# Weight forms kept over a change of token half, a down projection in alternating thirds, and new constants of the planner

## The chip, the cores and the metric

The kernel runs on one core of a Trainium2 chip. The metric is the device time of one execution in microseconds (us), given as the median of several runs. The engines are TensorE (PE, with its weight loads listed apart as PEld), VectorE (DVE), ScalarE (ACT), GpSimd (POOL) and SyncE (SP), which issues nearly all the DMAs of this kernel.

## The reference, cut to what matters

One decoder block over 2048 tokens and 1024 channels, in float32:

```python
u = rms_norm(h, norm1_gain)
x_lru, g_lru, q, k, v, g_ret = split(u @ w_in)            # 1024 x 3072
y_lru = rms_norm(rg_lru(conv4(x_lru)) * gelu(g_lru))      # a scan along the tokens
y_ret = head_group_norm(retention(rotary(q), rotary(k), v)) * silu(g_ret)
h = h + concat(y_lru, y_ret) @ w_out                      # 1024 x 1024
a, b = split(conv3(rms_norm(h, norm2_gain) @ ffn_up_w))   # 1024 x 6144, conv along the tokens
h = h + (gelu(a) * b) @ ffn_down_w                        # 3072 x 1024
return rms_norm(h, final_norm_gain)
```

## The kernel before, in words

**Tiling.** Activations are held transposed, channels on the 128 partitions and tokens along the free axis. The 2048 tokens are two halves of 1024 (`HT`), called g = 0 and g = 1. Work goes through stages: A and AS (input projection), B (output projection), U (up projection) and D (down projection, whose 3072 inputs are cut into three thirds, c = 0, 1, 2, each of which adds to the residual). `order` near the end of the kernel lists the stages: A and AS of half 0, AS of half 1, B of both halves, U of both, then the thirds 0, 1, 2 of D for half 0 and the thirds 0, 1, 2 for half 1.

**Units.** A stage is a list of units. A unit takes two weight tiles of 128 x 1024 (`wsrc`) and makes two output tiles of 128 x 1024. `PlainUnit` does this in eight products of twelve matmuls; `Unit` does it in seven, with sums and differences of weight quarters and of activation blocks (a Strassen form; `PRODUCTS` lists them). Each float32 operand is split into a high part (an ACT cast to fp32r) and a low part (a DVE subtraction), and each product sums high x high, high x low and low x high. `Unit.weights` loads the two tiles (`wa`, `wb`), forms the sums (`s`) on DVE, and splits them: it makes the forms a, s1, s2 and v, seven slots of 4 KB per partition. Every unit of every half does this afresh, so each weight tile is loaded and split twice, once per half. After a product that uses a form last, `free` gives its slots back. The last unit of the last stage is a `LastUnit`, a plain unit whose columns are cut finer at the end.

**Outputs.** A unit's sums leave PSUM through `PlainOut` (ACT copies; stages A and U) or `AddOut` (DVE additions onto a residual tile that was loaded; stages B and D). Then the chains of the stage go on: `LruOut` (conv, gates on TensorE, `pa` and `pg`, then sigmoid, exp, tanh, sqrt on ACT, a scan on DVE and, when all four LRU units of a half are done, `LruGroup` with the `mst` matmuls over `sqacc`), `QkOut` and `VgOut` (rotary and retention), `UpOut` (conv and gelu; two neighbouring channels j are put together in `even[0]` and written as blocks to DRAM), `NormGroup` (a norm over the eight output tiles of a half).

**What sets the order.** The program is written out by a planner in Python, `Flow`. Every chain is a generator that yields one engine operation at a time; the planner keeps a clock for each engine and for the DMAs with costs of its own, and at each step issues, on the engine that can start first, the ready operation of the lowest rank. The order on each engine is then fixed. Time is counted in ticks: each product of the main chain has a tick, a `Unit` has period 7. Its constants: `SOON` is by how many ticks a chain that empties PSUM is due earlier than its nominal time; `NEAR` and `RESERVE` hold back the last four SBUF slots (of `SLOTS` = 55) from chains that are due later; `BACKLOG` is how many us of DMA work may be queued; `XS` says how long ahead of a half its normalised input is made; `CL` stands in the rank:

```python
def rank(self, tick):
    return self.prio if self.feeds or tick > 10 ** 5 else max(self.prio, tick - CL)
```

`prio` is the due tick. The chains that feed TensorE (`main`, `bring`, `weights`) keep it. With CL = 100 practically every other chain keeps it too, so the longer one is overdue, the lower its rank and the sooner it goes.

**Around the change.** `ORDER` lists the units of stage A for each half: `l3` is LRU unit 3, `q0` and `v0` the two units of retention head 0. `stage_b`, `stage_u` and `stage_d` build the unit lists in ascending order for both halves. `Stage.bring` loads the activation blocks of a stage and splits them (`raw`, `bh`).

Of the kernel before, what the change touches and what calls it, by code (L numbers as in the profile page):

```python
# [32 lines left out]
KT = D // P  # L33
# [5 lines left out]
NF = DFF // P  # L39
# [1 line left out]
SLOTS = 55  # L41
BANKS = {"x": 1, "y": 2, "e": 2, "sm": 3}
RESERVE = 4
NEAR = 3
BACKLOG = 10.0
SMALL = 150
ORDER = ("l0 q0 v0 l1 q1 v1 l2 q2 v2 l3 q3 v3", "l0 q0 v0 l1 q1 v1 q2 v2 l2 q3 v3 l3")
RATE = 330.0
LATE = 16
PLAIN = 4  # L50
SOON = 1.5
WB = 2
CH = 4
ISSUE = 0.45
CL = 100
NDUE = 3
LESS = 0
XSTEP = 6
XD0 = 10
XS = 60  # L60
XD = 50
RAW = 4
LEAD = 12
# [264 lines left out]
def hymba_block_kernel(ctx: ExitStack, tc: tile.TileContext, xh, xn, win, wout, wup, down, gates, vecs,  # L328
# [3 lines left out]
    NG = S // HT  # L332
# [15 lines left out]
    free = fl.free  # L348
# [240 lines left out]
    class Unit:  # L589
# [6 lines left out]
        def __init__(self, stage, wsrc, out):  # L596
            self.stage, self.wsrc, self.out = stage, wsrc, out
            self.w = {}
            self.there = {n: Event() for n in ("a", "s1", "s2", "v")}
            self.done = {n: Event() for n in ("seed", "u2", "c11", "c22a", "c22b")}  # L600
            out.unit = self

        def weights(self, t0):
            self.t0 = t0
# [64 lines left out]
        def p1(self):  # L669
# [7 lines left out]

            fl.spawn(seed(), self.t0 - 3 - SOON)

# [8 lines left out]

        def p2(self):
            yield from self.product(self.x, "a", "12", "21", False)  # L690
            free(*self.w["a"])
            fl.spawn(self.out.c11(), self.t0 + 1.9 - SOON)

        def p7(self):
            yield self.done["u2"]
            yield from self.product(self.y, "s1", "3", "T3", False)
            free(*self.w["s1"])
            fl.spawn(self.out.c22(), self.t0 + 2.5 - SOON)

        def p4(self):  # L700
            yield self.done["c22a"]
            yield from self.product(self.y, "v", "v", "T4", False)
            free(self.w["v"])
            fl.spawn(self.out.c21(), self.t0 + 6 - LESS)

        def p3(self):
            yield self.done["c22b"]
            yield from self.product(self.e, "s2", "4", "22", False)
            free(*self.w["s2"])
            fl.spawn(self.out.c12(), self.t0 + 8 - LESS)  # L710

    class PlainUnit:


        period = 8
        quads = ((0, 0), (0, 1), (1, 0), (1, 1))
# [4 lines left out]
        def __init__(self, stage, wsrc, out):  # L721
            self.stage, self.wsrc, self.out = stage, wsrc, out
            self.w = {}
            self.there = [[Event(), Event()] for m in range(2)]
            self.placed = [Event(), Event()]
            out.unit = self
            out.quads = {}

# [48 lines left out]
        def part(self, q, m, n, k, c0=None, c1=None):  # L777
            if c0 is None:
                c0, c1 = n * Q, (n + 1) * Q
            if k == 0:  # L780
                PlainUnit.count += 1
                self.ps = yield Bank(self.tags[PlainUnit.count % 5], "pq")
            yield self.there[m][k]
            bname = f"{k + 1}{n + 1}"
            wh, wl = self.w[m]
            op = None
            for j in range(4):
                if j % 2 == 0:
                    yield self.stage.event(bname, j // 2)
                bh, bl = self.stage.blk[bname, j // 2]  # L790
                c = slice(j % 2 * Q + c0 - n * Q, j % 2 * Q + c1 - n * Q)
                ws = slice((4 * k + j) * P, (4 * k + j + 1) * P)
                for i, (x, y) in enumerate(((wh, bh), (wh, bl), (wl, bh))):
                    mm = pe.matmul(self.ps[:, 0:c1 - c0], x[:, ws], y[:, c], start=k == 0 and j == 0 and i == 0,
                                   stop=k == 1 and j == 3 and i == 2)
                    op = op + mm if op else mm
                if self.halves:
                    yield op
                    op = None
            if op:  # L800
                yield op
            self.stage.used(bname)
            if k == 1:
                if m not in [x[0] for x in self.quads[q + 1:]]:
                    free(*self.w[m])
                fl.spawn(self.leave(m, n, c0, c1), self.t0 + 2 * q + 4 - SOON)

        def leave(self, m, n, c0, c1):
# [665 lines left out]
    class UpOut(PlainOut):  # L1474
# [22 lines left out]
        def first(self):  # L1497
            t0 = self.unit.t0
            yield t0 + 11
            ca = yield from self.conv(self.t1, self.j)  # L1500
            yield a.activation(ca, ca, AF.Gelu_apprx_tanh)
            yield self.there
            yield v.tensor_tensor(out=ca, in0=ca, in1=self.cv, op=ALU.mult)
            free(self.cv)
            if self.j % 2 == 0:
                even[0] = ca
            else:
                yield t0 + 14
                yield from g_d[self.g][self.j // 8].put(self.j // 2 % 4, even[0], ca)

    even = [None]


    def stage_a(g):
# [24 lines left out]
    def stage_b(g):  # L1539
        st = RawStage("B", g, m_d[g])  # L1540
        ng = NormGroup(V_N2, u_d[g].put, h_d[g][0], LATE * g)
        us = []
        for m in range(KT // 2):
            ms = (m, m + KT // 2)
            src = [(x_d[g][k // 2], k % 2) for k in ms]
            us.append(PlainUnit(st, (wout[ms[0]], wout[ms[1]]), AddOut(src, lambda i, t, ms=ms: ng.add(ms[i], t))))
        return st, us

    def stage_u(g):
        st = Stage("U", g, u_d[g])  # L1550
        return st, [Unit(st, (wup[j], wup[NF + j]), UpOut(g, j)) for j in range(NF)]

    def stage_d(g, c):
        st = Stage("D", g, g_d[g][c])
        final = g == NG - 1 and c == 2

        def store(q, *pair):
            for j in range(2):
                m = 2 * q + j
                yield dma(yT[m * P:(m + 1) * P, g * HT:(g + 1) * HT], pair[j])  # L1560
                free(pair[j])

        ng = FinalGroup(V_NF, None) if final else NormGroup(V_NF, store, h_d[g][3])

        def partial(m, t):
            yield from h_d[g][c + 1][m // 2].put(m % 2, t)
            free(t)

        us = []
        for m in range(KT // 2):  # L1570
            ms = (m, m + KT // 2)
            src = [(h_d[g][c][k // 2], k % 2) for k in ms]
            done = (lambda i, t, ms=ms: ng.add(ms[i], t)) if c == 2 else (lambda i, t, ms=ms: partial(ms[i], t))
            out = AddOut(src, done)
            out.pieces = lambda i, t, c0, c1, ms=ms: ng.piece(ms[i], t, c0, c1)
            kind = LastUnit if final and m == KT // 2 - 1 else Unit
            us.append(kind(st, (down[c, ms[0]], down[c, ms[1]]), out))
        return st, us

    order = sum((stage_a(g) for g in range(NG)), []) + [stage_b(g) for g in range(NG)] + [stage_u(g) for g in range(NG)]  # L1580
    order += [stage_d(g, c) for g in range(NG) for c in range(3)]

    def vectors():
        yield dma(gain1, vecs[:, V_N1:V_N1 + KT], "a")
# [3 lines left out]
    with tc.manual_schedule():  # L1588
        fl.spawn(setup(), -60)
        fl.spawn(vectors(), -50)  # L1590
        fl.spawn(constants(), 3)
        table = {}
        end = 0
        last = None
        for i, (st, us) in enumerate(order):
            if last is PlainUnit and type(us[0]) is Unit:
                end += 4
            if st.kind == "A":
                norm1(0, -200, end + NDUE)
                make_x(0, 0, end + XD0)  # L1600
            elif st.kind == "AS" and st.g:
                norm1(st.g, end - 70, end - 60)
                make_x(st.g, end - XS, end - XD)
            for j, u in enumerate(us):
                if type(u) is PlainUnit and last is Unit:
                    end += 0
                elif type(u) is Unit and last is PlainUnit and j:
                    end += 4
                last = type(u)
                u.weights(end)  # L1610
                if isinstance(u.out, AddOut):
                    u.out.load(end)
                for dt, name, block in u.products:
                    assert end + dt not in table
                    table[end + dt] = getattr(u, name)
                    st.uses(block, end + dt)
                end += u.period
            st.prepare(STAGE_LEAD if i else 300)

        def main():  # L1620
            for tick in sorted(table):
                yield tick
                fl.tick = tick
                yield from table[tick]()
            fl.tick = 10 ** 6

        fl.spawn(main(), -4)
        fl.run()
# [69 lines left out]
```

## Time and profile before

| what | us |
|---|---|
| median of 3 runs | 2182.34 (2181.40 to 2182.86) |
| profiled execution, its own time | 2183.93 |
| its span, first to last instruction | 2182.1 |
| TensorE busy in it | 2152.2 |
| VectorE busy in it | 1764.3 |
| ScalarE busy in it | 1245.9 |

The profile is of one execution. In its views "busy" is the time in which an engine has an instruction at work; a row of waits names who waited, for whom, the us in total, how many times, and the longest; the granted clock is a share of TensorE's full 2.4 GHz, so 0.50 is 1.2 GHz. The chain of waits is followed back from the last instruction. Matmuls are pipelined: the mean duration of one is longer than the distance from one to the next.

### The profile page before, as it was taken

The numbers are of one execution on the slowest core, as the hardware profiler recorded it, in microseconds if no ns is written. First come the engines' busy times: TensorE is split into PE (matmuls) and PEld (weight loads), VectorE is DVE, ScalarE is ACT, GpSimd is POOL, SyncE is SP. The second block draws the span as 40 slices with busy tenths as digits, with TensorE's granted clock in tenths as the row PEclk, the third lists the DMA queues.
The fourth block names the chain that finished last, engine by engine and source line by source line (L and its number), as shares of the span: only waits on it lengthen the run. The fifth ranks groups of instructions, "written<-read, shape, count | busy, mean of one in ns | idle before, by whom it ended". The sixth has DMA issues, their size and how long they took to land.

```text
span 2182.1 us, 26589 instructions
## 1 busy us (share of the span) xinstructions
PE 2152.2 (99%) x9848; PEld 1773.1 (81%) x9848; DVE 1764.3 (81%) x2227; ACT 1245.9 (57%) x1792; POOL 39.3 (2%) x32
## 2 busy tenths in 40 slices
PE   9999989999999999999999999999999999999998
PEld 6878878888788888888888888888888788888787
DVE  6999888877765688898888898788878987788875
ACT  6774775654852166666666766666666553343441
POOL 0010000000000000000000000000000000000000
PEclk9999999999999999999999999999999999999999
DMA  8966365142647954453224532322335787689662
GB/s 323 373 228 207 109 222 167 61 137 70 224 164 263 374 191 167 166 177 130 100 91 155 193 121 97 116 90 97 112 118 177 264 314 254 227 295 398 230 255 78
DMA packets 142498, 411.00 MB, mean 188 GB/s; under 512 B 16112, under 2 KB 20640, under 8 KB 142368
## 3 DMA queue, kind: packets, MB, share of 16 engines
q1 hardware_dynamic: 141072, 408.25, 52.8%
q8 instruction: 77, 1.26, 0.2%
q10 hardware_dynamic: 1296, 1.05, 0.1%
q14 instruction: 53, 0.43, 0.1%
HBM read 275.78 MB, written 125.07 MB: 184 GB/s over the span
## 4 chain that ended last, share of the span: by engine, by line
PE 94%; DVE 3%; DMA 2%; ACT 1%; POOL 0%; issue 0%; SPq 0%; DVEq 0%
PE py L127 33%; PE px L127 22%; PE pe L127 22%; PE pq L127 12%; PE po L127 1%; DMA raw<-in_dram 1%; PE pa L127 1%; PE pt L127 1%; PE pk L127 1%; PE sc L127 1%; DVE raw L127 1%; PE mst L127 1%; DMA xt<-in_dram 0%; DVE res L127 0%; DMA h<-h 0%
## 5 line engine op out<-in xcount | busy, mean ns | idle before, releaser
L127 DVE TENSOR_TENSOR wl<-s,wh 128x1024 fp32r<-128x1024 f32 x182 | 222.2, 1221 | 108.8 <-ACT wh L127 106.5
L127 PE MATMUL px<-bh,wh 128*128 128x512 f32 x728 | 287.2, 395 | 0.4 <-DVE res L127 0.4
L127 PE MATMUL py<-bh,wl 128*128 128x512 f32 x728 | 284.0, 390 | 2.8 <-DVE wl L127 2.8
L127 PE MATMUL px<-raw,wh 128*128 128x512 f32 x728 | 285.0, 391 | 0.3 <-DVE raw L127 0.3
L127 PE MATMUL py<-bh,wh 128*128 128x512 f32 x728 | 285.2, 392 | 0.0
L127 PE MATMUL pe<-raw,wh 128*128 128x512 f32 x728 | 283.4, 389 | 1.6 <-DVE raw L127 1.6
L127 PE MATMUL pe<-bh,wh 128*128 128x512 f32 x728 | 284.8, 391 | 0.0
L127 PE MATMUL px<-bh,wl 128*128 128x512 f32 x728 | 284.7, 391 | 0.0
L127 PE MATMUL py<-raw,wh 128*128 128x512 f32 x728 | 283.8, 390 | 0.3 <-DVE raw L127 0.3
L127 PE MATMUL pe<-bh,wl 128*128 128x512 f32 x728 | 283.5, 389 | 0.0
L127 ACT CAST wh<-s 128x1024 fp32r<-128x1024 f32 x182 | 190.9, 1049 | 140.8 <-DVE s L127 127.2
L127 DVE SCALAR_TENSOR_TENSOR c<-o,vec,c 128x1022 f32<-128x1022 f32 x192 | 244.1, 1279 | 9.0 <-ACT c L127 4.6
L127 PE MATMUL py<-bh,wv 128*128 128x512 f32 x728 | 240.4, 391 | 3.4 <-ACT o L127 1.7
L127 ACT COPY o<-py 128x512 f32<-128x512 f32 x204 | 119.6, 587 | 198.1 <-PE py L127 197.7
L127 DVE TENSOR_TENSOR raw<-raw,bh 128x1024 fp32r<-128x1024 f32 x158 | 189.2, 1217 | 7.0 <-ACT bh L127 7.0
L127 ACT CAST bh<-raw 128x1024 fp32r<-128x1024 f32 x158 | 161.5, 1048 | 35.7 <-DMA raw<-g_T 14.4
L127 PE MATMUL pq<-bh,wh 128*128 128x512 f32 (+1 forms) x432 | 168.0, 389 | 0.5 <-ACT bh L127 0.4
L127 PEld LDWEIGHTS px<-bh,wh 128*128 128x128 f32 x728 | 137.8, 189 | 35.3 <-issue 3.8
L127 PE MATMUL pq<-bh,wl 128*128 128x512 f32 (+1 forms) x432 | 165.0, 382 | 0.5 <-DVE wl L127 0.5
L127 PEld LDWEIGHTS py<-bh,wv 128*128 128x128 f32 x728 | 136.7, 188 | 34.1 <-ACT o L127 2.2
L127 PEld LDWEIGHTS py<-bh,wl 128*128 128x128 f32 x728 | 136.8, 188 | 31.8 <-DVE wl L127 3.2
L127 PEld LDWEIGHTS px<-bh,wl 128*128 128x128 f32 x728 | 137.5, 189 | 29.0
(143 smaller groups left out, 3819.1 us busy)
## 6 DMA issues: line engine op xcount, KB each, us to landing
wa<-in_dram SPq DMA_DIRECT2D x91, 512.0 KB, 4.6
wb<-in_dram SPq DMA_DIRECT2D x91, 512.0 KB, 5.2
h<-res SPq DMA_DIRECT2D x56, 512.0 KB, 3.4
g_T<-t SPq DMA_DIRECT2D x96, 256.0 KB, 2.5
raw<-g_T SPq DMA_DIRECT2D x48, 512.0 KB, 7.0
res<-h SPq DMA_DIRECT2D x48, 512.0 KB, 7.7
g<-c SPq DMA_DIRECT2D x76, 256.0 KB, 3.4
raw<-g SPq DMA_DIRECT2D x38, 512.0 KB, 7.9
```

The source lines that it names most:

```text
L127: return Op(self.name, lambda: fn(*args, **kw), us, writes, reads, func=func)
```

## The change

Where two units that follow one another in different stages use the same weight tiles, the second takes over the first one's forms (`same`): its own `weights` is replaced by `begin`, which only notes its start, and the first one doesn't free them (`drop` with `keep`). The unit orders are changed so that the last unit of the first half to go and the first of the second have the same weights: `l3` in stage A, tile 3 in B, channel tiles 23 in U, and tile 3 in each third of D. The thirds of D now go half 0, half 1 (third 0), half 1, half 0 (third 1), half 0, half 1 (third 2). That makes six changes of half with kept forms: one in each of A, B and U and three in D. In U the pairing of channels goes by `twin` because 23 now comes before 22. Five constants change: NEAR, BACKLOG, SOON, CL and XS.

```diff
-NEAR = 3
-BACKLOG = 10.0
+NEAR = 5
+BACKLOG = 8.0
-ORDER = ("l0 q0 v0 l1 q1 v1 l2 q2 v2 l3 q3 v3", "l0 q0 v0 l1 q1 v1 q2 v2 l2 q3 v3 l3")
+ORDER = ("l0 q0 v0 l1 q1 v1 l2 q2 v2 q3 v3 l3", "l3 q0 v0 l0 q1 v1 q2 v2 l1 q3 v3 l2")
-SOON = 1.5
+SOON = 2.5
-CL = 100
+CL = 6
-XS = 60
+XS = 50
@@ class Unit
+            self.keep = False
+        def same(self, other):
+            self.w, self.there, self.weights = other.w, other.there, self.begin
+            other.keep = True
+        def begin(self, t0):
+            self.t0 = t0
+        def drop(self, *tiles):
+            if not self.keep:
+                free(*tiles)
@@ Unit.p2, p7, p4, p3 (one line each; here p2)
-            free(*self.w["a"])
+            self.drop(*self.w["a"])
@@ class PlainUnit
+        same, begin, drop = Unit.same, Unit.begin, Unit.drop
-                    free(*self.w[m])
+                    self.drop(*self.w[m])
@@ UpOut.first
-            if self.j % 2 == 0:
-                even[0] = ca
+            if not twin:
+                twin.append(ca)
             else:
                 yield t0 + 14
-                yield from g_d[self.g][self.j // 8].put(self.j // 2 % 4, even[0], ca)
+                even, odd = (twin.pop(), ca) if self.j % 2 else (ca, twin.pop())
+                yield from g_d[self.g][self.j // 8].put(self.j // 2 % 4, even, odd)
@@ stage_b
-        for m in range(KT // 2):
+        for m in (range(KT // 2) if g == 0 else reversed(range(KT // 2))):
@@ stage_u
-        return st, [Unit(st, (wup[j], wup[NF + j]), UpOut(g, j)) for j in range(NF)]
+        js = list(range(NF)) if g == 0 else [NF - 1, NF - 2, *range(NF - 2)]
+        return st, [Unit(st, (wup[j], wup[NF + j]), UpOut(g, j)) for j in js]
@@ stage_d
-        for m in range(KT // 2):
+        for m in (range(KT // 2) if g == c % 2 else (KT // 2 - 1, *range(KT // 2 - 1))):
-            kind = LastUnit if final and m == KT // 2 - 1 else Unit
+            kind = LastUnit if final and m == KT // 2 - 2 else Unit
@@ order and the loop over it
-    order += [stage_d(g, c) for g in range(NG) for c in range(3)]
+    order += [stage_d(g, c) for c in range(3) for g in (range(NG) if c != 1 else reversed(range(NG)))]
-        last = None
+        last = before = None
                 last = type(u)
+                if before and type(before) is last and [w.offset for w in before.wsrc] == [w.offset for w in u.wsrc] and \
+                        before.wsrc[0].tensor.name == u.wsrc[0].tensor.name:
+                    u.same(before)
+                before = u
                 u.weights(end)
```

## Rows read from the trace of the kernel before

**Rows 1.** The page's head: span, busy time of each engine.
```profile
span 2182.1 us, 26589 instructions
PE 2152.2 (99%) x9848; PEld 1773.1 (81%) x9848; DVE 1764.3 (81%) x2227; ACT 1245.9 (57%) x1792; POOL 39.3 (2%) x32
```

**Rows 2.** A window: length, busy PE, PEld, DVE, ACT, POOL, clock, DMA share, GB/s.
```profile
1000.00:1690.00 690.00, 690.00 (x3045) 571.34 (x3045) 574.14 (x635) 455.62 (x742) 0.00 (x0) 1.00 0.35 121
```

**Rows 3.** Waits of TensorE over the whole span, the longest of 14.
```profile
PE mst L127 <- DVE sqacc L127: 7.5, 2, 6.3
PE py L127 <- DVE wl L127: 2.8, 1, 2.8
...
PE py L127 <- ACT o L127: 1.7, 1, 1.7
PE py L127 <- DVE res L127: 1.7, 2, 0.9
PE pe L127 <- DVE raw L127: 1.6, 1, 1.6
...
PE px L127 <- DVE res L127: 0.4, 1, 0.4
```

**Rows 4.** The chain that ended last, in order of time: start, us, what.
```profile
125.01 4.54 PE px L127 x12
...
147.65 3.48 PE py L127 x10
151.13 3.46 PE px L127 x12
154.59 2.73 PE py L127 x12
...
316.69 3.54 PE mst L127 x16
320.24 4.26 PE px L127 x12
...
1944.57 1.68 PE mst L127 x16
```

**Rows 5.** Windows at the long wait, in the first unit of half 1.
```profile
310.00:316.60 6.60, 0.36 (x2) 0.00 (x0) 6.37 (x7) 6.20 (x8) 0.00 (x0) 0.72 0.44 143
316.60:323.00 6.40, 6.30 (x23) 5.75 (x24) 4.94 (x6) 2.47 (x3) 2.01 (x1) 0.50 0.28 111
```

**Rows 6.** Groups by form, weight work: count, busy us, mean ns, idle before.
```profile
L127 DVE TENSOR_TENSOR wl<-s,wh 128x1024 fp32r<-128x1024 f32 x182 | 222.2, 1221 | 108.8 <-ACT wh L127 106.5 <-DMA h<-res 1.3 <-PE px L127 0.4
L127 ACT CAST wh<-s 128x1024 fp32r<-128x1024 f32 x182 | 190.9, 1049 | 140.8 <-DVE s L127 127.2 <-PE pe L127 7.7 <-PE px L127 3.6
...
L127 DVE TENSOR_TENSOR s<-wb 128x512 f32<-128x512 f32 x91 | 62.1, 683 | 3.2 <-PE px L127 1.5 <-DMA wb<-in_dram 1.1 <-DMA out_dram<-h 0.6
...
L127 ACT CAST wv<-wb 128x512 fp32r<-128x512 f32 x91 | 56.3, 618 | 9.2 <-DMA h<-res 2.9 <-DVE sqacc L127 2.6 <-DVE o L127 2.2
```

**Rows 7.** DMA issues: what, count, KB each, median us to landing.
```profile
wa<-in_dram SPq DMA_DIRECT2D x91, 512.0 KB, 4.6
...
h<-res SPq DMA_DIRECT2D x56, 512.0 KB, 3.4
...
res<-h SPq DMA_DIRECT2D x48, 512.0 KB, 7.7
```

**Rows 8.** Windows of one unit each, before and after the change of half in A.
```profile
289.00:310.00 21.00, 21.00 (x94) 16.31 (x92) 14.34 (x14) 19.89 (x24) 0.00 (x0) 1.00 0.98 318
310.00:331.00 21.00, 14.66 (x65) 12.38 (x64) 19.25 (x21) 11.84 (x16) 2.01 (x1) 0.76 0.36 123
```

**Rows 9.** Windows in D: after half 0's end, and two near the end.
```profile
1953.00:1972.00 19.00, 18.64 (x82) 15.10 (x81) 13.81 (x17) 2.59 (x3) 0.00 (x0) 1.00 0.99 355
...
2105.00:2124.00 19.00, 19.00 (x86) 15.73 (x85) 11.69 (x14) 7.29 (x8) 0.00 (x0) 1.00 0.40 138
2124.00:2143.00 19.00, 18.22 (x81) 14.77 (x80) 8.75 (x10) 4.01 (x4) 0.00 (x0) 1.00 0.00 1
```

More of the change, by code (lines that the diff above doesn't have):

```diff
@@ L696, in p7 @@
             yield from self.product(self.y, "s1", "3", "T3", False)
-            free(*self.w["s1"])
+            self.drop(*self.w["s1"])
             fl.spawn(self.out.c22(), self.t0 + 2.5 - SOON)
@@ L702, in p4 @@
             yield from self.product(self.y, "v", "v", "T4", False)
-            free(self.w["v"])
+            self.drop(self.w["v"])
             fl.spawn(self.out.c21(), self.t0 + 6 - LESS)
@@ L708, in p3 @@
             yield from self.product(self.e, "s2", "4", "22", False)
-            free(*self.w["s2"])
+            self.drop(*self.w["s2"])
             fl.spawn(self.out.c12(), self.t0 + 8 - LESS)
     class PlainUnit:
+        same, begin, drop = Unit.same, Unit.begin, Unit.drop
         period = 8
@@ L725, in __init__ @@
             self.placed = [Event(), Event()]
+            self.keep = False
             out.unit = self
@@ L1504, in first @@
             free(self.cv)
-            if self.j % 2 == 0:
-                even[0] = ca
+            if not twin:
+                twin.append(ca)
             else:
                 yield t0 + 14
-                yield from g_d[self.g][self.j // 8].put(self.j // 2 % 4, even[0], ca)
-    even = [None]
+                even, odd = (twin.pop(), ca) if self.j % 2 else (ca, twin.pop())
+                yield from g_d[self.g][self.j // 8].put(self.j // 2 % 4, even, odd)
+    twin = []
     def stage_a(g):
```

## The prediction

> **What bounds the kernel now.** I read the page's head first, then windows over the whole span, then TensorE's waits, then the chain that ended last. The head shows TensorE busy for 2152.2 of 2182.1 us [rows 1], so at most 29.9 us of idle are there to be had, the start and the tail among them. A long window in the up projection shows what the kernel is like where nothing is wrong: 690 us without a gap at the full clock, 3045 matmuls, 0.227 us from one to the next [rows 2]. A product of twelve then takes 2.72 us and a `Unit` of seven products 19.0 us. The change adds and removes no matmul of the products. It can only win what TensorE loses against that pace, and I list those losses by place.
>
> The waits [rows 3] name them. The largest by far is one wait of 6.3 us of `mst` for `sqacc` (the other of that row is at the end of the kernel). It lies right behind the change of half in stage A [rows 5]: DVE is busy for 6.37 of 6.60 us and ACT for 6.20, so both are working off a queue while TensorE, in order, stands at a small matmul that nobody needs yet. Behind it the granted clock is 0.50, 1.2 GHz. The chain of waits prices that: the sixteen `mst` matmuls take 3.54 us where sixteen take 1.68 at the full clock, and the next product 4.26 where one takes 2.73 [rows 4]. The place costs 6.3 + 1.9 + 1.5 = 9.7 us. In the first AS units the same happens in small: a wait of 2.8 us for `wl` [rows 3], and half-clock stretches in which products take 4.54, 3.48 (ten matmuls) and 3.46 us [rows 4], 1.8 + 1.2 + 0.7 = 3.7 us too much; together 6.5. Next are waits for a PSUM bank that ACT or DVE had not emptied: `py` for `o` 1.7, `py` for `res` 1.7 in two, `px` for `res` 0.4, in all 3.8 us [rows 3]; and one wait of 1.6 for an activation block at the start of D [rows 3]. That makes 9.7 + 6.5 + 3.8 + 1.6 = 21.6 us in the middle of the kernel. The rest of the idle is start and tail, which the change doesn't touch.
>
> A rule of the Trainium skill gives another headroom. Its page Perfetto Trace Analysis, section Identifying the Most-Contended Engine, says that matmul busy time is no good measure and that the busy share of LDWEIGHTS is to be read: 81% here, which would leave a fifth of the span, some 400 us (an estimate from that page's rule). The trace disagrees as to the size: in the gapless window LDWEIGHTS is busy for 571.34 of 690 us, 82.8% [rows 2], so that is this kernel's full pace, and 1773.1 / 0.828 = 2141 us [rows 1] is the span without a loss, start and tail included.
>
> **The change part by part.** *Kept forms.* At a change between two `Unit`s fall away two loads of 512 KB [rows 7], three low parts at 1.22 us, four half-size sums and one half-size low at about 0.68 on DVE, three casts at 1.05 and one at 0.62 on ACT [rows 6]: 7.1 us of DVE, 3.8 us of ACT. Five such changes and the plain one in B (two lows, two casts, the same sizes) make 38 us of DVE, 21 us of ACT and twelve loads. Almost all of it lies beside matmuls: in the up projection DVE is 83% busy and TensorE never waits [rows 2], so in B and U it brings nothing. It counts where DVE is behind. At the change in A it is behind by those 6.3 us, and the 7.1 us of DVE and 3.8 of ACT that go are due in the units just before and after. That is more than the wait. Slots: the seven kept slots are held one unit longer, but the second set of seven and the three raw slots aren't taken, so nothing is tighter.
>
> *Order of units in A.* `l3` moves to the end of half 0 and the start of half 1, so the end of the LRU group, with the `mst` matmuls, moves back by about two units, and two LRU units stand side by side. In the unit's length in which the gates of `l3` run now, ACT is busy for 19.89 of 21 us; in the next DVE for 19.25 of 21 [rows 8]. Two ACT stretches in a row less the kept 3.8 us are 36 of 42 us, so they still fit; the DVE stretch less up to 7.1 falls to 12 to 19 of 21. I take it that the wait goes to the size of an ordinary one, 1.7 us [rows 3], with no fall of the clock: gain 8.0. Bounds: 9.7 if it goes wholly, a loss of 9.7 if the second LRU unit meets a wait like it. The value is near the first because the work removed exceeds the wait.
>
> *Thirds alternate.* The norm of half 0, with eight loads and eight stores of 512 KB and eight DVE steps, runs now at the start of half 1's thirds, where the DMA share is 0.99 and TensorE loses 0.4 us [rows 9]. It moves into the last third of half 1, into the stretch 2105 to 2143, in which the DMA share is 0.40 and 0.00 and DVE is busy for 11.69 and 8.75 of 19 us [rows 9]; ten us of DVE fit, and about 40 us remain to the end, so the tail stays as it is. If that cover were gone, the last stores would add their landing time, some 3 to 8 us [rows 7]. A residual written by one third is read by the next third of that half three units later instead of four: 57 us against a store of 3.4 and a load of 7.7 [rows 7], no cost unless both take five times as long. Gain 0.4 with the `px` wait, which I count with the banks.
>
> *SOON.* Chains that empty a bank are due a tick (2.72 us) sooner, ahead of the cast of the next unit's first weight, which had the same due tick. Each of the 3.8 us of bank waits is shorter than a tick. I take 3.0 of 3.8; bounds 3.8 and, because weight splits then come later, a loss of 2.8 as in the one `wl` wait [rows 3].
>
> *CL.* Chains that don't feed TensorE and are more than six ticks (16 us) overdue lose their advantage over each other and over feeding chains that are later still. No row shows how far a chain is overdue. It costs nothing where none is that late, wins up to the 2.8 + 1.6 us of waits for `wl` and `raw` [rows 3], and loses up to another 6.3 where a small matmul in TensorE's order belongs to such a chain. I take 0, nearest to the long window without a wait [rows 2].
>
> *NEAR, BACKLOG, XS.* Slots are granted two ticks earlier, the DMA queue is planned 2 us shallower, the input of half 1 is made 10 ticks (27 us) later. Weight loads are asked for 12 ticks ahead and land in 4.6 us [rows 7]; the input is ready some 30 ticks ahead and its blocks are fetched 20 ahead. All lie inside cover, cost 0; without it each late load costs a wait of the 1.6 us kind [rows 3].
>
> *Pairing and reversed lists* change no work. The first AS units and the start of D have no kept forms near: their 6.5 and 1.6 us stay.
>
> Sum: 8.0 + 3.0 = 11.0 us. The profiled execution is 2183.93 us (its span and 1.8 around it), 1.6 above the median of the runs, so I take the gain off the median: 2182.3 - 11.0 = 2171.3, forecast 2171. Its own range: from everything named being won but the early waits (9.7 + 3.8 + 1.6: 2167), further down to 2163 if the early waits shrink by half their 6.5 too, up to 2178 if only part of the A wait goes.
>
> **The rivals.** *The wait comes back where the group now ends.* The plan again puts `mst` on TensorE before `sqacc` is there, a unit or two later. For it: the wait arises from the planner's clocks running ahead of the chip, not from the weights, and the four ops from the last scan to `sqacc` stand in the same full queues [rows 5]. Against it: less work ahead of it. Only 3 us of banks are won, less one new small wait of 1.6: 2181, between 2178 and 2187.
>
> *Two LRU units side by side are too much* (slower). Place: the first two units of half 1. The gate matmuls and the end of the group need ACT and DVE twice in succession; when ACT's 36 of 42 us [rows 8] become more than 42, that is when 6 us of other chains fall there, TensorE stands in order at `pa` or `mst`. Price: the old 9.7 stays and another comes with its half-clock stretch, less 2 us of bank waits: 2182.3 + 9.7 - 2 = 2190, between 2187 and 2200. For it: 95% of ACT in one unit's length. Against it: the low ACT share, 11.84 of 21, in the next [rows 8].
>
> *All waits go.* The new ranks also clear the early units: 2182.3 - 21.6 = 2161, down to 2157.
>
> *The change doesn't do what it says.* The comparison of offsets matches fewer than six pairs; then `wa` stays above 86 issues and the time goes as in the first rival. By the lists all six match, so I give it no more than a part of that rival's chance.
>
> **How the numbers follow.** Forecast 0.55; the wait comes back 0.20; too much side by side 0.17; all waits go 0.08. A measurement of this kernel can tell about 0.2% from no change, 4.4 us: faster is under 2178, slower above 2186.7. Faster gets the first and the last, 0.63, less 0.01 for the upper edge: 0.62. Same gets the second, with that edge and a little of its neighbours: 0.21. Slower 0.17. The range goes from 2160 to 2189: it leaves out the lower half of the last case, 0.04, and a bit over half of the slower case, 0.10.
>
> **What would show it right or wrong.** `wa` and `wb` with 86 issues each instead of 91, and DVE's busy time down by about 38 us. In TensorE's waits the `mst` row without its 6.3 and no half clock between 300 and 370 us: the A step is right; a wait of `mst`, `pa` or `pg` of more than 3 us there: one of the first two rivals. Waits for `o` and `res` under 1 us in total: the SOON step. The stores of half 0's result between about 2095 and 2150 us and a tail unchanged to 1 us: the step on the thirds. The forecast is wrong if new waits appear in U or D, which have hardly any now: then the ranks or the slots matter more than I gave them.

## The result, and the profile after

| | before | after |
|---|---|---|
| median of 4 runs, us | 2182.60 (2181.40 to 2183.58) | 2166.56 (2165.12 to 2168.05) |
| profiled execution and its span, us | 2183.93, 2182.1 | 2167.17, 2165.3 |
| ratio of the times | | 0.9922, 95% interval 0.9909 to 0.9934 |

The change makes the kernel 16.0 us faster by these medians, 0.73%; the ratio on record, 0.9922, is 0.78%, and both lie within its interval. 11 us were forecast. The page's head, and the DMA issues that answer to [rows 7] (what, count, KB each, median us to landing):

```profile
span 2165.3 us, 26460 instructions
PE 2143.6 (99%) x9848; PEld 1768.5 (82%) x9848; DVE 1729.8 (80%) x2185; ACT 1226.1 (57%) x1768; POOL 38.3 (2%) x32
...
wa<-in_dram SPq DMA_DIRECT2D x86, 512.0 KB, 4.4
```

Against [rows 1] TensorE has the same 9848 matmuls, DVE 34.5 us and ACT 19.8 us less to do (38 and 21 were forecast), and `wa` is loaded 86 times for 91, which is five changes of half. The sixth, with plain units in B, loads `w`: 23 tiles of 512 KB for 25. So all six keep their forms. TensorE's waits, answering to [rows 3]:

```profile
PE px L127 <- DVE raw L127: 1.8, 1, 1.8
...
PE px L127 <- DVE res L127: 1.4, 1, 1.4
PE py L127 <- DVE wl L127: 1.3, 2, 1.0
PE mst L127 <- DVE sqacc L127: 1.2, 1, 1.2
PE py L127 <- DVE res L127: 1.0, 1, 1.0
...
PE py L127 <- ACT o L127: 0.8, 2, 0.4
```

No wait is longer than 1.8 us; the `mst` wait left is the one at the kernel's end. The stretches answering to [rows 5], first the early AS units, then the place of the long wait (length, then busy PE, PEld, DVE, ACT, POOL, then clock, DMA share, GB/s), and the `mst` matmuls of half 0 in the chain, which now run at 359 us:

```profile
120.00:152.00 32.00, 30.18 (x134) 23.09 (x133) 31.56 (x38) 23.39 (x32) 0.72 (x1) 1.00 0.49 163
300.00:323.00 23.00, 23.00 (x138) 20.24 (x137) 20.13 (x46) 10.64 (x14) 1.82 (x1) 1.00 0.16 52
```

```profile
359.40 1.68 PE mst L127 x16
```

The granted clock is 1.00 where it was 0.50, and the sixteen `mst` take 1.68 us where they took 3.54 [rows 4].

**Where the time went.** To compare many runs I need one number per place. For each matmul I take the time to the next one's start, less the undisturbed pace: 0.2266 us for a full product matmul (690 / 3045 [rows 2]), the median of its kind for the others. Summed over a stretch, this is what TensorE lost there, by waits and by half clock together. In all fourteen traces the span less the whole loss is 2134.8 to 2136.2 us, so the table accounts for the spans. All in us; "half clock" is how long the granted clock was 0.50 between the start and the end of the kernel; "ratio" is against runs of before on the same chip.

| kernel | 0 to 100 | 100 to 290 | 290 to 450 | 450 to 1690 | 1690 to 2110 | rest | sum | half clock | ratio, 95% |
|---|---|---|---|---|---|---|---|---|---|
| before | 8.9 | 11.1 | 11.7 | 5.1 | 5.8 | 4.0 | 46.6 | 17.1 | |
| after | 8.0 | 7.1 | 4.6 | 3.5 | 3.2 | 3.9 | 30.2 | 0 | 0.9922 (0.9909 to 0.9934) |
| constants_only | 7.6 | 7.1 | 17.3 | 3.8 | 5.5 | 3.7 | 44.9 | 17.1 | 0.9995 (0.9986 to 1.0005) |
| structure_only | 8.4 | 10.6 | 9.8 | 5.1 | 2.5 | 6.8 | 43.3 | 13.7 | 0.9985 (0.9975 to 0.9994) |
| no_kept | 7.8 | 8.5 | 12.0 | 3.8 | 2.7 | 4.5 | 39.3 | 6.8 | 0.9972 (0.9961 to 0.9983) |
| mst_later | 7.7 | 11.0 | 9.7 | 15.3 | 4.8 | 3.7 | 52.2 | 20.5 | 1.0038 (1.0025 to 1.0051) |
| soon_back | 8.0 | 18.0 | 6.3 | 5.6 | 2.2 | 5.4 | 45.6 | 13.7 | 0.9996 (0.9986 to 1.0005) |
| near_back | 8.0 | 11.5 | 9.8 | 4.8 | 2.6 | 6.4 | 43.0 | 6.8 | 0.9996 (0.9986 to 1.0005) |
| replan_before | 8.6 | 8.3 | 12.5 | 4.9 | 5.4 | 3.7 | 43.4 | 17.1 | 0.9997 (0.9987 to 1.0006) |
| replan_after | 8.4 | 7.0 | 3.4 | 4.3 | 2.6 | 4.2 | 29.8 | 0 | 0.9922 (0.9907 to 0.9937) |
| keep_in_A | 8.2 | 6.7 | 3.4 | 3.8 | 2.6 | 4.7 | 29.4 | 0 | 0.9930 (0.9916 to 0.9945) |
| keep_not_in_A | 7.7 | 7.1 | 11.8 | 3.8 | 1.7 | 4.0 | 36.1 | 3.4 | 0.9955 (0.9940 to 0.9970) |
| plain_thirds | 8.3 | 6.0 | 3.4 | 3.6 | 6.2 | 3.7 | 31.3 | 0 | 0.9943 (0.9928 to 0.9958) |
| pair_v3 | 8.0 | 6.4 | 11.1 | 3.1 | 1.8 | 3.9 | 34.2 | 6.8 | 0.9959 (0.9945 to 0.9973) |

From before to after the loss falls by 16.4 us: 7.1 around the change of half in A, 4.0 in the early AS units, 2.6 in D, 1.6 from 450 to 1690, 1.0 at start and end. The trace is of one execution of each kernel, so the columns tell where time went, and the ratios tell whether a kernel is faster.

### The profile page after: what moved, and what is told of

Its sections match the earlier page's. It is cut to its first block, busy times and chain, and to the rows that moved or that the text cites. A ratio compares the mean times of both kernels' runs of the same rounds, so it can differ in the third digit from the quotient of the medians.

```text
span 2165.3 us, 26460 instructions
## 1 busy us (share of the span) xinstructions
PE 2143.6 (99%) x9848; PEld 1768.5 (82%) x9848; DVE 1729.8 (80%) x2185; ACT 1226.1 (57%) x1768; POOL 38.3 (2%) x32
## 4 chain that ended last, share of the span: by engine, by line
PE 92%; DVE 3%; DMA 3%; issue 1%; ACT 0%; SPq 0%; POOL 0%; DVEq 0%; ACTq 0%
PE py L127 33%; PE px L127 22%; PE pe L127 21%; PE pq L127 12%; PE po L127 1%; DMA raw<-in_dram 1%; PE pa L127 1%; PE pk L127 1%; PE sc L127 1%; PE pt L127 1%; DVE o L127 0%; PE mst L127 0%; DMA xt<-in_dram 0%; DMA x<-in_dram 0%; DVE wl L127 0%
## 5 line engine op out<-in xcount | busy, mean ns | idle before, releaser
L127 DVE TENSOR_TENSOR wl<-s,wh 128x1024 fp32r<-128x1024 f32 x172 | 210.2, 1222 | 113.4 <-ACT wh L127 108.7
L127 ACT CAST wh<-s 128x1024 fp32r<-128x1024 f32 x172 | 180.4, 1049 | 122.1 <-DVE s L127 107.1
L127 PEld LDWEIGHTS py<-bh,wh 128*128 128x128 f32 x728 | 136.7, 188 | 33.1 <-issue 3.0
L127 PEld LDWEIGHTS px<-bh,wh 128*128 128x128 f32 x728 | 136.7, 188 | 31.3 <-DVE res L127 1.8
```

The costliest lines, as they stand in the source:

```text
L127: return Op(self.name, lambda: fn(*args, **kw), us, writes, reads, func=func)
```

## The experiments

Theory 1, as I went in: the kept forms take DVE work away just where DVE is behind, and that removes the wait in A; the constants only shorten bank waits. Rival: the constants re-plan the order, and that is what does it.

**constants_only.** The kernel before with the five constants:

```diff
-NEAR = 3, BACKLOG = 10.0, SOON = 1.5, CL = 100, XS = 60
+NEAR = 5, BACKLOG = 8.0, SOON = 2.5, CL = 6, XS = 50
```

> The kernel before with the five new constants alone; orders, loads and splits as before. Theory 1 (the kept forms remove the wait in A; the constants only shorten bank waits): 2179 us, the 6.3 us wait of mst still there with its half clock, the waits for o and res under 1 us. Rival (the constants re-plan the order and the waits go with that): under 2173 us, no mst wait and no half clock in the middle, although DVE still does all 1764 us of work.

2182.59 us, ratio 0.9995: no measurable difference, so the rival alone is out, and theory 1, which expected 2179, misses too. In the table the early AS units improve from 11.1 to 7.1, as in the full change, but from 290 to 450 us the loss grows to 17.3: 11.0 at the change of half (before: 10.1 up to 331 us), and 6.3 behind it, where a wait for `wl` near 388 us is new. Its waits from 290 to 420 us, and two windows there:

```profile
PE py L127 <- DVE raw L127: 5.0, 1, 5.0
PE py L127 <- DVE wl L127: 2.9, 1, 2.9
```

```profile
304.00:312.00 8.00, 3.27 (x10) 2.43 (x10) 7.93 (x8) 7.70 (x10) 0.00 (x0) 0.64 0.47 147
312.00:320.00 8.00, 8.00 (x27) 6.64 (x27) 6.54 (x9) 1.90 (x3) 2.54 (x1) 0.51 0.15 62
```

It is no longer `mst` that waits but a product, for a low part of an activation block. DVE is full as before, 7.93 of 8 us.

**structure_only.** The changed kernel with the five old constants (the diff above the other way round).

> The changed kernel with the five old constants: kept forms, new unit orders and alternating thirds alone. Theory 1: 2172 us, the wait of mst gone, bank waits of about 3.8 us as before, early half clock (6.5 us) as before. Rival (the constants do it): 2178 us or more, with a wait of mst, pa or wl over 3 us in A.

2180.34 us, ratio 0.9985: 3.6 us below the 2183.9 of before beside it, not the 10 of theory 1. The wait after the change of half is gone, but another comes at 375 us with its half clock; its longest wait in that stretch and the product behind it in the chain:

```profile
PE py L127 <- ACT o L127: 5.4, 2, 4.1
```

```profile
374.68 4.60 PE py L127 x12
```

So neither half of the change is worth much, and the gain is theirs together.

**no_kept.** The changed kernel without its kept forms:

```diff
-                    u.same(before)
+                    pass
```

> The changed kernel, but each unit loads and splits its own weights again (91 loads of wa); orders, thirds and constants as in the change. Theory 1: 2175 us, since the 7.1 us of DVE at the change in A are back and a wait of several us with half clock comes with them. Rival (the order and the constants do it, the kept forms lie beside matmuls): 2167 to 2169 us, DVE busy 38 us more, no wait over 3 us.

2177.06 us, ratio 0.9972: the kept forms are worth about 10 us, as theory 1 said. But not where it said. The place of the old wait, 300 to 325 us, is clean without them too (0.2 us of loss). The loss comes 25 to 50 us later, in the first units of half 1:

```profile
PE py L127 <- ACT o L127: 5.2, 2, 3.5
```

ACT's timeline there, without kept forms (start, us, what, and in brackets the idle before it):

```profile
332.21 1.05 ACT L127 CAST wh<-s 128x1024 fp32r<-128x1024 f32 x1 [3.50 <-DVE s L127]
333.28 1.28 ACT L127 ACT_TABLE_LOAD   x1
334.57 0.69 ACT L127 ACTIVATE tt<-pa,vec 64x512 f32<-64x512 f32 x1
...
338.02 1.05 ACT L127 CAST wh<-s 128x1024 fp32r<-128x1024 f32 x1
...
341.80 0.59 ACT L127 COPY o<-px 128x512 f32<-128x512 f32 x1
342.41 1.28 ACT L127 ACT_TABLE_LOAD   x1
343.70 1.15 ACT L127 ACTIVATE ea<-tt,m8sp 128x1024 f32<-128x1024 f32 x1
344.89 1.15 ACT L127 ACTIVATE tt<-tt,m4sp 128x1024 f32<-128x1024 f32 x1
346.06 1.28 ACT L127 ACT_TABLE_LOAD   x1
347.35 1.06 ACT L127 ACTIVATE tt<-tt 128x1024 f32<-128x1024 f32 x1
348.31 0.57 ACT L127 COPY o<-py 128x512 f32<-128x512 f32 x1
```

And in the changed kernel:

```profile
329.85 1.28 ACT L127 ACT_TABLE_LOAD   x1
331.14 0.68 ACT L127 ACTIVATE tt<-pa,vec 64x512 f32<-64x512 f32 x1
...
340.57 0.59 ACT L127 COPY o<-py 128x512 f32<-128x512 f32 x1 [0.72 <-PE py L127]
341.18 1.28 ACT L127 ACT_TABLE_LOAD   x1
342.48 1.15 ACT L127 ACTIVATE ea<-tt,m8sp 128x1024 f32<-128x1024 f32 x1
```

This is the wait, seen whole. An LRU unit has a block of two table loads and three activations, 5.9 us on ACT (342.41 to 348.31). A copy that empties a bank can stand before the block or behind it. In the changed kernel the copy of `py` comes at 340.57, just before; without kept forms the gates start 3.4 us later (334.57 for 331.14), behind a cast of the weights at 332.21 with 3.5 us of idle for its DVE sum, and with another cast among them; the copy lands behind the block, at 348.31, and TensorE waits 3.5 us for the bank, then runs a stretch at half clock. In structure_only the copy that ended the wait of 4.1 us, at 374.06, stands behind such a block too, 368.15 to 374.06.

**mst_later.** The kernel before, with the LRU group's matmuls later in the order:

```diff
             if self.ss.left == 0:
+                yield Until(fl.tick + 7)
                 r = yield Slot("rb")
```

> The kernel before with one line more: the chain of the LRU group waits seven ticks (about 19 us) before its mst matmuls, so that they stand later in TensorE's order. No work is removed. If the 9.7 us at that place are only the early place of a small matmul in the order: 2173 us and no wait of mst in A. If DVE's backlog is the cause, TensorE waits there for something else (a low part of weights, an activation block) and the time stays within 3 us of 2182.

2192.02 us, ratio 1.0038, slower. At the change of half the loss falls only from 11.7 to 9.7, and another instruction takes over the wait (290 to 330 us):

```profile
PE px L127 <- DVE raw L127: 4.4, 1, 4.4
```

So `mst` was not the cause: what waits here is whatever needs DVE's work next. The extra 10 us lie from 675 to 725, in B: the line also holds back the group of half 1, and the `mst` of the next norm then meet a wait of their own, with 10.2 us of half clock:

```profile
693.85 1.92 PE L127 MATMUL mst<-ones,sqacc 128*128 128x1 f32 x16 [3.22 <-DVE sqacc L127]
```

How the one leads to the other was not tested.

Theory 2, formed on these four: three things are needed together. The unit order moves `l3`'s DVE work away from the change of half; the kept forms and an earlier emptying of PSUM clear the pair of LRU units that this order makes. The next four runs test it, two of them against chance: the planner is a list scheduler, and any constant moves hundreds of instructions.

**soon_back.** The changed kernel with one constant back:

```diff
-SOON = 2.5
+SOON = 1.5
```

> The changed kernel with SOON back at 1.5, all else as in the change. Theory 2 (three parts are needed together: the order and the kept forms clear the change in A, and chains that empty PSUM must come a tick earlier because two LRU units stand side by side on ACT): a wait of py for o of 3 to 4 us with half clock comes back between 340 and 380 us, 2172 us. Rival (NEAR and the queue's depth did it, by when loads come): 2167 us and no such wait.

2183.00 us, ratio 0.9996: the whole gain is gone. A wait for `o` does come back at the pair (`px`, 3.2 us), but the larger loss is at 225 to 247 us, where no version had one:

```profile
PE py L127 <- DVE wl L127: 4.4, 1, 4.4
PE py L127 <- ACT wh L127: 2.5, 1, 2.5
```

```profile
225.00:236.00 11.00, 9.02 (x40) 6.68 (x36) 5.04 (x6) 10.39 (x12) 0.00 (x0) 1.00 0.16 48
236.00:247.00 11.00, 6.08 (x14) 4.37 (x15) 10.79 (x10) 4.00 (x6) 0.00 (x0) 0.54 0.26 88
```

First ACT is full (10.39 of 11 us) and DVE half idle, then DVE is full (10.79) and ACT idle: a cast of the weights came late on ACT (235.45, behind the block of another LRU unit, 229.55 to 235.45), and the low parts after it bunch up on DVE. Theory 2 foresaw the direction and a third of the size; the place it did not. Nor is it shown that SOON as such guards this place: structure_only has SOON at 1.5 as well, with the other four old constants, and loses 0.2 us there.

**near_back.** Likewise `NEAR = 3` in place of 5.

> The changed kernel with NEAR back at 3, all else as in the change. Theory 2: the early AS units, which the five constants together brought from 8.7 to 2.9 us of loss, keep that, and the time stays at 2167 us. Rival (slots granted two ticks earlier let loads and splits of the early units come sooner): the wait of 2.8 us for wl with its half clock is back before 155 us, 2172 us or more.

2183.19 us, ratio 0.9996: again nothing of the gain is left in the medians; its profiled execution was 2180.31. The loss from 290 to 450 is that of structure_only, 9.8, with the same wait for `o` of 4.1 us, and the early units are back at 11.5. They are not as before, though: up to 155 us they lose 4.6 (before 10.0, the change 3.2), and 3.1 more come from 225 to 290 us, with a wait of 1.7 for `y`. So with the rest as it is the gain needs both SOON and NEAR. Theory 2, which expected 2167, is wrong on NEAR. The rival here named the early units, where half clock is indeed back, but not the change of half.

**replan_before** and **replan_after.** The two kernels with `RATE = 331.0` in place of 330: planned DMAs are 0.3% faster and no work changes, but part of the order does. In the traces some 90 to 220 instructions of ACT's and 130 to 170 of DVE's about 2,200 and 2,700 stand elsewhere, fewer than 50 of TensorE's 9848. It is a mild shake.

> The kernel before with one cost of the planner moved by 0.3% (RATE 331 for 330), which re-orders instructions and changes no work. If losses are what the plan meets by chance, it lies several us from 2183 either way; if they belong to the structure, within 2 us of it, with the wait of mst after the change in A still there.

> The changed kernel with the same 0.3% on RATE. If the gain of 16 us belongs to the parts of the change, within 3 us of 2167; if it is one lucky plan among many, 2172 us or more, with a new wait over 3 us somewhere in A.

2182.66 us (0.9997) and 2166.76 us (0.9922). The losses at the change of half stand: 12.5 and 3.4 for 11.7 and 4.6. In replan_before it is not `mst` that waits there but

```profile
PE py L127 <- DVE raw L127: 5.3, 1, 5.3
```

which is the same lesson as mst_later. So the gain survives a second order on either side, and the change of half in A isn't luck. The early units are less firm: in replan_before, with all old constants, they lose 8.3 for 11.1.

**keep_in_A** and **keep_not_in_A.** Kept forms at the change in A alone, and everywhere but there:

```diff
-                    u.same(before)
+                    if st.kind == "AS":      # keep_not_in_A: != "AS"
+                        u.same(before)
```

> The changed kernel with kept forms only at the change of half in A; B, U and D load and split anew at each change. Theory 3 (the kept forms count only where ACT is behind, which is the pair of LRU units in A): 2167 to 2169 us, no wait over 2 us between 290 and 450 us. Rival (they count in D as well): 2172 us, with new waits after 1700.

> The changed kernel with kept forms in B, U and D but not in A, where both halves load and split l3's weights. Theory 3: 2175 to 2177 us, as without any kept forms, with the 3.5 us wait of py for o and half clock between 325 and 375. Rival: 2170 us or less.

2168.36 us (0.9930) and 2173.46 us (0.9955). With A alone the loss is 29.4 us, the full change's 30.2, and the intervals overlap: five of the six kept sets do nothing that shows. Without A the stretch from 290 to 450 loses 11.8, as in no_kept, with the same 3.5 us wait for `o`. The time is a little under the expected 2175 to 2177, with an interval that overlaps that of no_kept.

**plain_thirds.** The changed kernel with D in the old order, and so with no kept forms there (two more lines put the tiles and the `LastUnit` back):

```diff
-    order += [stage_d(g, c) for c in range(3) for g in (range(NG) if c != 1 else reversed(range(NG)))]
+    order += [stage_d(g, c) for g in range(NG) for c in range(3)]
```

> The changed kernel with the down projection as before: all three thirds of half 0, then those of half 1, tiles in ascending order, no kept forms in D; everything else as in the change. If the alternating thirds are worth what the rows of before said (the norm of half 0 out of a full DMA queue): 2168 to 2169 us, with small waits back between 1930 and 2030. If they do more: over 2171. If nothing: 2166.5.

2171.32 us, ratio 0.9943. The alternation is worth 3.0 us by the loss in D (6.2 for 3.2), 4.8 by the medians, with overlapping intervals. Over all fourteen traces it is plain: the five with the old order of D lose 4.8 to 6.2 us there, the nine with the alternating one 1.7 to 3.2. The waits from 1900 to 2060 and a window show the place that [rows 9] named:

```profile
PE px L127 <- DVE raw L127: 1.7, 1, 1.7
PE py L127 <- DVE res L127: 0.7, 1, 0.7
```

```profile
1955.00:1975.00 20.00, 19.31 (x86) 15.66 (x85) 15.97 (x20) 5.20 (x6) 0.00 (x0) 1.00 1.01 380
```

**pair_v3.** Theory 2 blames the pair of LRU units for what the kept forms must clear. So another order with kept forms, but without the pair:

```diff
-ORDER = ("l0 q0 v0 l1 q1 v1 l2 q2 v2 q3 v3 l3", "l3 q0 v0 l0 q1 v1 q2 v2 l1 q3 v3 l2")
+ORDER = ("l0 q0 v0 l1 q1 v1 l2 q2 v2 l3 q3 v3", "v3 q3 l0 q0 v0 l1 q1 v1 l2 q2 v2 l3")
```

> The changed kernel with other lists for A: half 0 ends with l3 q3 v3 as before, half 1 begins v3 q3 l0, so the kept forms are those of v3 and no two LRU units stand side by side at the change. If the pair of LRU units is what puts ACT late: the loss between 290 and 400 us (3.7 in the change) falls under 1.5 and the time is 2163 to 2165 us. Rival (the end of the LRU group one unit earlier brings the wait of mst back): 2175 us or more, with a wait of mst or of an activation block near 310 us.

2174.00 us, ratio 0.9959, between the two that were expected. With `l3` two units before the change again, the old place loses 4.3 us (300 to 325 us), although 7.1 us of DVE are kept off: TensorE waits 2.1 us at 309.5 us for `raw`. A larger loss, 5.6 us, comes from 420 to 450 us, where TensorE waits 3.5 us for `wl`. The waits from 290 to 450 us, then two windows at the old place:

```profile
PE px L127 <- DVE wl L127: 3.5, 1, 3.5
PE py L127 <- DVE raw L127: 2.1, 1, 2.1
```

```profile
300.00:310.00 10.00, 7.92 (x34) 6.22 (x33) 8.98 (x8) 8.62 (x11) 0.00 (x0) 0.98 0.41 144
310.00:316.00 6.00, 6.00 (x30) 5.10 (x29) 5.00 (x7) 2.84 (x4) 0.14 (x1) 0.74 0.07 30
```

The kept forms alone do not clear that place; the position of `l3` does. From 300 to 325 us the nine traces with `l3` last lose 0.1 to 0.3 us, the five with `l3` earlier 4.3 to 10.7. That the pair of LRU units is what costs the rest isn't shown by this run, since it brings a loss of its own later on. None of these versions is better than the change.

**CL.** With 100 put back, the changed kernel's program comes out the same, instruction for instruction on every engine; so does the kernel before with 6. This constant changes nothing, so there was nothing to run.

## Why the prediction was right, point by point

The direction and the main place were right, for partly the wrong reason; the size was short by 5 us. That it came no further off is in part luck: of SOON's 3.0 us hardly any came where it was expected, and 9.2 of the 16.4 us lie in places to which the sum gave nothing or 0.4.

*What bounds the kernel.* Right: TensorE's loss against the undisturbed pace is all that moved. The span less the loss is the same within 1.4 us in all runs. But the list of losses was too short: 21.6 us in the middle of the kernel, where the table has 33.7 between 100 and 2110 us. The page Perfetto Trace Analysis of the Trainium skill (Identifying the Most-Contended Engine) has the busy share of LDWEIGHTS, beside the share of peak FLOP/s, as the measure. Scaled to the busy share of a gapless window, 0.828, it gives 2136 us for the span without loss after (1768.5 / 0.828), where the table has 2135.1; from the trace of before it gave 2141, where the table has 2135.5.

*The A step* was forecast at 8.0 us and gave 7.1: the old place lost 10.1 us (290 to 331) and now loses 0.5, and behind it the loss grew from 1.6 to 4.0. The cause named for the wait was half wrong. That the wait is for DVE was right; that TensorE stands "at a small matmul that nobody needs yet" was where the wait shows, not why: moved away, it passes to an activation block. And "the work removed exceeds the wait" was not what cleared it. no_kept is clean there with all the work; pair_v3 is not, with the work kept off. What clears it is that `l3`'s chain comes later than the change of half. DVE is not emptier for it; the same window as in [rows 5], in the changed kernel:

```profile
310.00:316.60 6.60, 6.60 (x36) 5.61 (x35) 6.39 (x14) 2.64 (x4) 0.00 (x0) 1.00 0.31 102
```

DVE is busy for 6.39 of 6.60 us, as before, and TensorE doesn't wait. So "DVE is busy" doesn't make a wait; what stands in its queue ahead of TensorE's next operand does. The kept forms act one to two units later, where the copy of a bank stands behind the LRU block on ACT. They do so through both engines: without them the gates come 3.4 us later, and before them ACT stands idle for 3.50 us, for a DVE sum of weights (332.21).

*The pair of LRU units* was the slower rival, and its mechanism is real: structure_only, near_back, no_kept and keep_not_in_A all show it, as a wait for `o` of 3.5 or 4.1 us with half clock. It named `pa` or `mst` as what would wait; it is a bank. With the kept forms, SOON and NEAR together the waits there stay at 0.9 us or less.

*SOON* was forecast at 3.0 of 3.8 us of bank waits. They hardly fell: 0.8 for `o`, 1.0 and 1.4 for `res`, 3.2 us in all. Yet without SOON the gain is gone. The step failed in looking only at the waits that the kernel before had: in soon_back the lost time lies at 225 to 247 us and at the pair, where the kernel before has no such wait. Whether SOON acts there as it was meant to, or by the order that happens to come with it, isn't shown.

*NEAR, BACKLOG, XS at 0* is the term most mis-sized. Without NEAR's step nothing is left of the gain; and with the five constants together the early AS units went from 11.1 to 7.1 us, which I had left untouched at their 6.5. Those 4.0 us are most of what the forecast lacked. Whose they are isn't shown. Up to 155 us the loss is 10.0 in before and 9.7 in structure_only, 4.0 in constants_only and 3.2 in the change, so the five constants do bring it. But it is 4.6 with SOON or NEAR alone put back, 4.6 in no_kept with all five new ones, and 4.5 in replan_before with all five old ones: a changed order can win most of it by itself. BACKLOG and XS were not tried alone.

*CL at 0* was right, more strictly than argued.

*Thirds* were forecast at 0.4 us and are worth about 3, by the medians up to 5: the norm of half 0 costs more in a full DMA queue than the one wait beside it showed, since loads for the next units are late as well (`raw` 1.7). The last stores do fit before the end: half 0's result is written from 2099.5 to 2117.2 us, and the loss after 2110 is 3.9 for 4.0. With NEAR at 3 the end isn't as clear: structure_only and near_back lose 6.8 and 6.4 there, with waits for `res` of 1.8 and 3.2 us.

```profile
L365 SPq DMA_DIRECT2D out_dram<-h x8: 332/338/433, 2099.5 to 2117.2; - x8
```

*Kept forms in B, U and D at 0* was right: keep_in_A.

## What to carry to other kernels

In a kernel whose busiest engine has no work to lose, list its losses against its own undisturbed pace by place, and ask for each place what stands ahead of TensorE's next operand in which queue; the instruction that waits can be only the first in line, and here moving it moved the wait. A queue that is full isn't yet a loss. Reuse of loaded operands paid at one of six places here, the one where the work that it saves stood ahead of the emptying of a bank. A change of order and the priorities it is planned with have to be tried together: each half alone gave 0 to 0.15%, both gave 0.78%.

## What the runs showed of the hardware

The granted clock fell after shorter waits than I had expected, and not after every wait. In the kernel before it is down from 125 us on, where TensorE had just waited 0.9 us, between eight transposes and four gate matmuls of 64 rows (PE's timeline, then a window):

```profile
120.06 2.07 PE L127 MATMUL py<-idt,y 128*128 128x128 f32 x8
123.03 1.12 PE L127 MATMUL pa<-xc,ea 64*128 64x512 f32 x2 [0.91 <-DVE xc L127]
123.89 1.12 PE L127 MATMUL pg<-xc,ea 64*128 64x512 f32 x2
```

```profile
125.00:129.00 4.00, 4.00 (x12) 3.14 (x12) 4.00 (x6) 2.21 (x4) 0.00 (x0) 0.57 0.60 211
```

In the changed kernel a wait of 1.8 us leaves it at 1.00, and there is no half clock between its start and its end. The same wait can go either way. In near_back and in the changed kernel TensorE runs the same stretch of matmuls around 120 us and stands for 1.82 us at the same one, 0.11 us apart by the clock of the trace; the granted clock falls in the one and not in the other (first near_back, then the changed kernel):

```profile
122.78 0.50 PE L127 MATMUL px<-raw,wh 128*128 128x512 f32 x1 [1.82 <-DVE raw L127]
124.00:127.00 3.00, 3.00 (x10) 1.38 (x8) 3.00 (x5) 1.87 (x3) 0.00 (x0) 0.51 0.38 157
...
122.67 0.51 PE L127 MATMUL px<-raw,wh 128*128 128x512 f32 x1 [1.82 <-DVE raw L127]
124.00:127.00 3.00, 3.00 (x15) 1.85 (x14) 3.00 (x5) 1.97 (x3) 0.00 (x0) 1.00 0.54 221
```

So half clock that one version has and another has not need not come from a wait that only the one has. In the kernel before, the 6.3 us of wait were followed by another 3.4 us lost to matmuls at 1.2 GHz, so this wait cost half as much again.
